# A hybrid decoder layer: the level products of three recurrent heads on 64-column halves of the array

## The chip, the core and the metric

One core of a Trainium2 chip runs the whole layer as one program. Its engines work side by side, each through its own queue in order: TensorE (matrix products; PE in the profile, its weight loads PEld), VectorE (DVE), ScalarE (ACT), GpSimd (POOL) and SyncE (SP), which issues most DMAs. The metric is the device time of the program in microseconds, median of three runs. Lower is better.

## The reference, cut to what matters

The layer is a mixer (eight heads of dilated attention beside four heads of a gated linear recurrence) and a feed-forward block. The change is in the recurrence. For one head and chunks of 64 positions:

```python
def step(state, xs):
    qc, kc, vc, gc = xs
    b = jnp.cumsum(gc, axis=2)
    o_inter = jnp.einsum('bhtk,bhkv->bhtv', qc * jnp.exp(b), state)
    diff = b[:, :, :, None, :] - b[:, :, None, :, :]
    decay = jnp.exp(jnp.where(causal, diff, -jnp.inf))
    a = jnp.einsum('bhtk,bhsk,bhtsk->bhts', qc, kc, decay)
    o = o_inter + jnp.einsum('bhts,bhsv->bhtv', a, vc)
    ...
```

The matrix `a` holds, for each query t and each earlier key s of its chunk, their product weighted by the decay between them, which differs in each of the 128 dimensions. There are 1024 positions, 128 dimensions a head, and everything is float32.

## The kernel before, in words

Positions are taken in eight tiles of 128, so that a tile holds two chunks of 64. The kernel keeps queries `qt` and keys `kt` of a head with the dimensions on the partitions and the positions along the row, and `tot`, the decay of each position.

**The levels.** The decayed products are not built one pair at a time. At level c the positions are cut in blocks of c. The products between the second block of each pair of blocks (queries) and the first (keys) are one matrix product, after which the queries and keys are multiplied by the decay of the block that they must now reach across. Levels 1, 2, 4, ... 32 fill a chunk, level 64 couples the two chunks of a tile, and the state carries what is further back.

Heads 0 to 2 take two levels, c and 2c, in one step, with c = 1, 4, 16 (`hgrn_core`, L502). For a step `quarter_sets` (L470) builds three sets of 64 queries a tile: one for level c, one for level 2c with the far half of the keys, one for the near half. Side by side they are the 192 columns of `qs`. One product a tile takes the tile's 128 keys as stationary operand and these 192 columns as moving operand (L529), and gives `pl`, 128 keys by 192 queries, in PSUM: eight products a step, two tiles to a bank. A key of the first chunk meets queries of both chunks there, and only those of its own chunk at the right blocks are wanted. DVE picks them out with `copy_predicated` (L561) into `at`, a table of 128 keys by 128 queries a tile, by masks: `masks` for the two levels, `near` for the set that couples at the smaller distance. Both masks are made once, near the start (L379 to L383), on DVE. `near` is followed there by `lb` and, by way of ACT, by the gates of head 0.

`at` begins as the diagonal (L511: the identity times a row of sums from `pd`). Level 64 is a product of its own, on 64 keys (L572), which ACT copies into the upper right quarter of `at` (L574). Then `at` is the stationary operand of the product that gives the head's output (L643). The last head takes the levels one by one (L593, L604).

**What sets the order.** The program is written out by hand: each engine runs its instructions in the order in which the code issues them. Projections of the next head (`pig`, `pm_q`, `pm_f`) and of the attention (`pm_aq`) stand in a queue of generators. Between the parts of a head, `fill(ns)` takes matrix products from it until the nanoseconds written there are used up. After each step it is called twice with 3500 times a scale. Between them `table_part` loads parts of the bias tables and turns them on POOL (`tout`, L718, L720). PSUM has eight banks in four pairs ("mm", "s", "t", "pv"); before, the four banks of `pl` of a step come from two of these pairs, in turn.

The masks come from an input of seven levels (`mraw`); `lowhalf` says for each key and step whether it lies in the second block at level c, and `near` is the mask of level 2c for those keys alone.

Of the kernel before, what the change touches and what calls it, by code (L numbers as in the profile page):

```python
# [10 lines left out]
U8 = mybir.dt.uint8  # L11
AF = mybir.ActivationFunctionType
# [25 lines left out]
def hymba_layer(ctx, tc, x, w_in, w_out, w_ff1, w_ff2, g_pre, lb_logits, g_mix, g_post,  # L38
# [26 lines left out]

    ident = cp.tile([P, P], F32, name="ident")
    masks = cp.tile([P, len(LEVELS), 64], U8, name="masks")
    near = cp.tile([P, 3, 64], U8, name="near")
    gpre = cp.tile([P, NK], F32, name="gpre")
    lbl = cp.tile([P, HH, 2], F32, name="lbl")  # L70
    lb = cp.tile([P, HH], F32, name="lb")
# [197 lines left out]
    def new_head(h):  # L269
        return {"inat": slab("T", f"inat{h}", F32, (P, NT, P)), "gate": slab("T", f"gate{h}", F32, (P, NT, P))}  # L270

    heads = [None] * HH
    heads[0] = new_head(0)

# [101 lines left out]
    for q in (2, 3):  # L376
# [3 lines left out]
    first = col("lowhalf", 3)  # L380
    V.tensor_reduce(first, mraw[:, 0:6].rearrange("p (s two) j -> p s two j", two=2)[:, :, 0], axis=AX.X, op=ALU.max)
    V.tensor_scalar(first, first, -1.0, 1.0, op0=ALU.mult, op1=ALU.add)
    V.tensor_tensor(out=near, in0=mraw[:, 0:6].rearrange("p (s two) j -> p s two j", two=2)[:, :, 1],  # L383
                    in1=first.unsqueeze(2).to_broadcast([P, 3, 64]), op=ALU.mult)
    V.tensor_tensor(out=lb, in0=lbl[:, :, 0], in1=lbl[:, :, 1], op=ALU.subtract)
    S.activation(omlb, lb, AF.Sigmoid, scale=-1.0)
    S.activation(lb, lb, AF.Sigmoid)
# [113 lines left out]
    def hgrn_core(h, scale, after=None):  # L501
# [5 lines left out]
        for hf in range(2):  # L507
            pd = bank("pv", f"pd{h}_{hf}")
            for q in range(2):
                TE.matmul(pd, ones.to_broadcast([P, P]), prod[q][:, hf * 512:hf * 512 + 512], start=q == 0, stop=q == 1)  # L510
            V.tensor_tensor(out=at[:, hf * 4:hf * 4 + 4], in0=ident.unsqueeze(1).to_broadcast([P, 4, P]),  # L511
                            in1=pd.rearrange("p (n c) -> p n c", n=4), op=ALU.mult)
        if h == 0:
            make_picks()
            nc.sync.dma_start(out=gcols, in_=g_mix.rearrange("(k p) -> p k", p=P))
# [2 lines left out]
        if h < HH - 1:  # L518
            fill(1200 * scale)
            totals = slab("P", f"tot{h}")  # L520
            for step in range(3):
                c = 4 ** step
                nb = 32 // c
                sets, cv = ready
                banks4 = []
                for u in range(4):
                    pl = bank(("s", "t", "pv")[(2 * step + u // 2) % 3], f"pl{h}_{step}{u}").rearrange("p (n q) -> p n q", n=2)
                    for n in range(2 * u, 2 * u + 2):
                        TE.matmul(pl[:, n % 2, :192], kt[:, n * P:(n + 1) * P], sets[u // 2][:, n % 4],  # L529
                                  start=True, stop=True)  # L530
                    banks4.append(pl)
                w = T // (4 * c)
                at_ = (0, 768, 960)[step]
                tots = totals[:, at_:at_ + 3 * w].rearrange("p (i w) -> p i w", i=3)
                u23, u123, nx = (tots[:, i] for i in range(3))
                cw = cv.rearrange("p n b f -> p (n b) f")
                q4 = qt.rearrange("p (m f c) -> p m f c", f=4, c=c)
                k4 = kt.rearrange("p (m f c) -> p m f c", f=4, c=c)

                def spread(ap, k=c):  # L540
                    return ap.unsqueeze(2).to_broadcast([P, w, k])
                V.tensor_tensor(out=q4[:, :, 1], in0=q4[:, :, 1], in1=spread(cw[:, :, 0]), op=ALU.mult)
                for hf in range(2):
                    n4 = slice(hf * 4, hf * 4 + 4)
                    V.tensor_tensor(out=qt[:, hf * 512:hf * 512 + 512].rearrange("p (n b f c) -> p n b (f c)", n=4, f=4, c=c)
                                    [:, :, :, 2 * c:],
                                    in0=sets[hf][:, :, 128:].rearrange("p n (b w) -> p n b w", b=nb),
                                    in1=cv[:, n4, :, 0:1].to_broadcast([P, 4, nb, 2 * c]), op=ALU.mult)
                V.tensor_tensor(out=u23, in0=cw[:, :, 2], in1=cw[:, :, 3], op=ALU.mult)
                V.tensor_tensor(out=u123, in0=cw[:, :, 1], in1=u23, op=ALU.mult)  # L550
                V.tensor_tensor(out=nx, in0=cw[:, :, 0], in1=u123, op=ALU.mult)
                if step < 2:
                    ready = quarter_sets(hd, h, step + 1, nx)
                V.tensor_tensor(out=k4[:, :, 2], in0=k4[:, :, 2], in1=spread(cw[:, :, 3]), op=ALU.mult)
                V.tensor_tensor(out=k4[:, :, 1], in0=k4[:, :, 1], in1=spread(u23), op=ALU.mult)
                V.tensor_tensor(out=k4[:, :, 0], in0=k4[:, :, 0], in1=spread(u123), op=ALU.mult)
                for u, pl in enumerate(banks4):
                    for part_, mask, c2 in ((0, masks[:, 2 * step], c), (2, masks[:, 2 * step + 1], 2 * c),
                                            (1, near[:, step], 2 * c)):
                        av = at[:, 2 * u:2 * u + 2].rearrange("p n (b two c) -> p n b two c", two=2, c=c2)  # L560
                        V.copy_predicated(  # L561
                            av[:, :, :, 1, :],
                            mask.rearrange("p (b c) -> p b c", c=c2).unsqueeze(1).to_broadcast([P, 2, 64 // c2, c2]),
                            pl[:, :, part_ * 64:part_ * 64 + 64].rearrange("p n (b c) -> p n b c", c=c2))
                cur = nx
                table_part()
                fill(3500 * scale)
                table_part()
                fill(3500 * scale)
            pl = bank("s", f"pl{h}_6")  # L570
            for n in range(NT):
                TE.matmul(pl[:64, n * 64:(n + 1) * 64], kt[:, n * P:n * P + 64], qt[:, n * P + 64:(n + 1) * P],  # L572
                          start=True, stop=True)
            S.activation(at[:64, :, 64:], pl[:64].rearrange("p (n c) -> p n c", n=NT), AF.Copy)  # L574
            kv, qv = (x.rearrange("p (n two c) -> p n two c", two=2, c=64) for x in (kt, qt))
            cv = cur.rearrange("p (n two) -> p n two", two=2)
            V.tensor_tensor(out=qv[:, :, 1], in0=qv[:, :, 1], in1=cv[:, :, 0:1].to_broadcast([P, NT, 64]), op=ALU.mult)
            V.tensor_tensor(out=kv[:, :, 0], in0=kv[:, :, 0], in1=cv[:, :, 1:2].to_broadcast([P, NT, 64]), op=ALU.mult)
            nx = tp.tile([P, NT], F32, tag="tot8", name=f"tot{h}_8", bufs=1)
            V.tensor_tensor(out=nx, in0=cv[:, :, 0], in1=cv[:, :, 1], op=ALU.mult)  # L580
            cur = nx
            fill(3400 * scale)
        else:
            cur = tot
            fill(1200 * scale)
            for li, c in enumerate(LEVELS):
                nb = 64 // c
                qv = qt.rearrange("p (b two c) -> p b two c", two=2, c=c)
                kv = kt.rearrange("p (b two c) -> p b two c", two=2, c=c)
                av = at.rearrange("p n (b two c) -> p n b two c", two=2, c=c)  # L590
                pl = bank("s", f"pl{h}_{li}")
                for n in range(NT):
                    TE.matmul(pl[:, n * 64:(n + 1) * 64], kt[:, n * P:(n + 1) * P],  # L593
                              qv[:, n * nb:(n + 1) * nb, 1, :], start=True, stop=True)
                w = T // (2 * c)
                cv = cur[:, :2 * w].rearrange("p (b two) -> p b two", two=2)
                V.tensor_tensor(out=kv[:, :, 0, :], in0=kv[:, :, 0, :],
                                in1=cv[:, :, 1:2].to_broadcast([P, w, c]), op=ALU.mult)
                V.tensor_tensor(out=qv[:, :, 1, :], in0=qv[:, :, 1, :],
                                in1=cv[:, :, 0:1].to_broadcast([P, w, c]), op=ALU.mult)  # L600
                nx = slab("P", f"tot{h}_{w}") if w > 32 else \
                    tp.tile([P, w], F32, tag=f"tot{w}", name=f"tot{h}_{w}", bufs=1)
                V.tensor_tensor(out=nx[:, :w], in0=cv[:, :, 0], in1=cv[:, :, 1], op=ALU.mult)
                V.copy_predicated(  # L604
                    av[:, :, :, 1, :],
                    masks[:, li].rearrange("p (b c) -> p b c", c=c).unsqueeze(1).to_broadcast([P, NT, nb, c]),
                    pl.rearrange("p (n b c) -> p n b c", n=NT, c=c))
                cur = nx
                fill((3700 if li == 0 else 2900 if li < 3 else 2200) * scale)
# [57 lines left out]
            gated(g2)  # L667


    halves = ((0, 64), (64, 128))  # L670
    pairs = [None] * (AH // 2)
    v_dram = [dp.tile([DIL, T // DIL, 4 * 64], F32, name=f"vd{pr}") for pr in range(AH // 2)]
    table_dram = [dp.tile([P, 4 * P + FAR], F32, name=f"tabd{hd}") for hd in range(AH)]
# [1638 lines left out]
```

## Time and profile before

| what | value |
|---|---|
| time, median of 3 runs | 1205.64 us (1205.62 to 1205.76) |
| the profiled execution: span from first to last instruction | 1203.5 us (the page gives no other time for it) |
| granted TensorE clock, mean | 0.999 |
| level products L529, PE | 144 records, 68.4 to 213.5 us |
| level-64 products L572, PE | 48 records, 99.0 to 222.2 us |
| masked copies L561, DVE | 108, 76.1 to 218.2 us |
| POOL and ACT busy | 294.7 us and 542.3 us |

How to read it: a float32 product of 128 by 192 appears as two matmul records and two weight loads (144 records for 72 products). A row of the timeline gives the start, the time until the last one's end, the engine, the line, the operation, what it writes and reads, and how many were merged. In "128*128 128x192" the first pair is the rows and columns of the array that the stationary operand takes, the second the moving operand. The ends of matmuls are modelled, so the distances between starts say more than the durations. In square brackets stands the idle time of the engine before the row, and what ended it.

### The profile page before, as it was taken

The page shows a single profiled execution, that of the slowest core. Times are in us where ns is not written, and L with a number is a line of the kernel's source. Part 1 is how long each engine was busy: PE and PEld are TensorE (multiplying, and loading weights), DVE is VectorE, ACT ScalarE, POOL GpSimd, SP SyncE. Part 2 cuts the span into 40 slices and gives each one's busy share as a digit, 9 for nine tenths or more (in the row PEclk, how much of TensorE's full clock was granted, in tenths as well). Part 3 has the DMA queues.
Part 4 walks back from the last instruction along what each step waited for, and adds up shares of the span by engine and source line. Part 5 has one row for each costly group of instructions (what it writes and reads, how often), then busy time and mean ns, then how long its engine had stood idle before and what let it go on. Part 6 is the DMA issues. An engine that isn't in the chain of part 4 may idle for free.

```text
span 1203.5 us, 17310 instructions
## 1 busy us (share of the span) xinstructions
PE 1195.3 (99%) x6342; PEld 1025.7 (85%) x6342; DVE 849.7 (71%) x1438; ACT 542.3 (45%) x1065; POOL 294.7 (24%) x280
## 2 busy tenths in 40 slices
PE   9999999999999999999999999999999999999997
PEld 9898989888888888888888888888888888888886
DVE  5696978775666767676599665766687553578796
ACT  7633333321565668855664222222234543434562
POOL 0121112010111110153421787575531000000022
PEclk9999999999999999999999999999999999999999
DMA  5222323135545556272524465553587534523337
GB/s 218 71 68 84 96 85 95 50 100 123 156 107 129 130 150 153 57 244 103 192 75 163 165 229 184 182 206 135 201 326 269 183 105 140 173 89 105 105 105 279
DMA packets 90547, 175.46 MB, mean 146 GB/s; under 512 B 14944, under 2 KB 42464, under 8 KB 90464
## 3 DMA queue, kind: packets, MB, share of 16 engines
q1 hardware_dynamic: 90320, 174.37, 45.6%
q8 instruction: 50, 0.82, 0.3%
q14 instruction: 33, 0.27, 0.1%
q10 hardware_dynamic: 144, 0.00, 0.0%
HBM read 116.91 MB, written 47.99 MB: 137 GB/s over the span
## 4 chain that ended last, share of the span: by engine, by line
PE 96%; ACT 2%; DVE 1%; issue 1%; DMA 0%; POOL 0%; DVEq 0%; POOLq 0%; ACTq 0%
PE f L2052 18%; PE f2s L2052 7%; PE pig L92 2%; PE pig L90 2%; PE pig L91 2%; PE pl L529 2%; PE pwo L90 2%; PE pwo L92 2%; PE pwo L91 2%; PE pm_ak L90 1%; PE pm_aq L90 1%; PE pm_f L90 1%; PE pm_aq L92 1%; PE pm_ak L92 1%; PE pm_ak L91 1%; PE pm_aq L91 1%
## 5 line engine op out<-in xcount | busy, mean ns | idle before, releaser
L87 DVE TENSOR_TENSOR al<-ar,ah 128x1024 fp32r<-128x1024 f32 x56 | 70.6, 1261 | 80.4 <-ACT ah L86 80.2
L2052 PE MATMUL f<-bh,ah 128*128 128x512 f32 x320 | 124.5, 389 | 0.0
L2052 PE MATMUL f<-bl,ah 128*128 128x512 f32 x320 | 124.5, 389 | 0.0
L2052 PE MATMUL f<-bh,al 128*128 128x512 f32 x320 | 124.5, 389 | 0.0
L86 ACT ACTIVATE ah<-ar 128x1024 fp32r<-128x1024 f32 x56 | 59.1, 1056 | 86.6 <-DMA ar<-actd 84.3
L2052 PEld LDWEIGHTS f<-bl,ah 128*128 128x128 f32 x320 | 60.1, 188 | 12.6
L2052 PEld LDWEIGHTS f<-bh,al 128*128 128x128 f32 x320 | 60.1, 188 | 12.5
L2052 PEld LDWEIGHTS f<-bh,ah 128*128 128x128 f32 x320 | 60.1, 188 | 12.3
L2126 POOL TENSOR_SCALAR lbl<-ssq 128x1 f32<-128x1 f32 x4 | 3.3, 820 | 245.7 <-ACT fd L2122 245.5
L1675 POOL TENSOR_TENSOR e<-x,e 128x512 f32<-128x512 f32 x14 | 21.6, 1541 | 131.0 <-DVE x L1626 123.8
L2052 PE MATMUL f2s<-bl,ah 128*128 128x512 f32 (+1 forms) x128 | 48.9, 382 | 0.0
L2052 PE MATMUL f2s<-bh,al 128*128 128x512 f32 (+1 forms) x128 | 48.9, 382 | 0.0
L2052 PE MATMUL f2s<-bh,ah 128*128 128x512 f32 (+1 forms) x128 | 48.9, 382 | 0.0
L718 POOL TENSOR_SCALAR tout<-traw 128x256 f32<-128x256 f32 x16 | 18.4, 1150 | 107.0 <-DMA traw<-in_bias_tab_dram 107.0
L87 DVE TENSOR_TENSOR bl<-br,bh 128x1024 fp32r<-128x1024 f32 x32 | 40.1, 1253 | 1.3 <-ACT bh L86 1.2
L2069 ACT ACTIVATE acc<-f 128x512 f32<-128x512 f32 x28 | 16.7, 598 | 49.5 <-PE f L2052 49.5
L86 ACT ACTIVATE bh<-br 128x1024 fp32r<-128x1024 f32 x32 | 33.6, 1050 | 4.3 <-PE f L2052 2.7
L87 DVE TENSOR_TENSOR wl<-raw,wh 128x1024 fp32r<-128x1024 f32 x21 | 25.9, 1233 | 10.2 <-ACT wh L86 10.2
L764 POOL TENSOR_TENSOR kl<-kf,kh 64x512 fp32r<-64x512 f32 x12 | 15.4, 1287 | 70.9 <-ACT kh L763 49.4
L90 PE MATMUL pwo<-woh,mt 128*128 128x512 f32 x80 | 32.2, 402 | 0.0
L92 PE MATMUL pwo<-woh,mt 128*128 128x512 f32 x80 | 31.3, 391 | 0.0
L91 PE MATMUL pwo<-wol,mt 128*128 128x512 f32 x80 | 31.2, 390 | 0.0
(1724 smaller groups left out, 3937.7 us busy)
## 6 DMA issues: line engine op xcount, KB each, us to landing
ar<-actd SPq DMA_DIRECT2D x56, 512.0 KB, 3.6
br<-in_w_ff_dram SPq DMA_DIRECT2D x16, 1024.0 KB, 5.8
raw<-in_w_in_dram SPq DMA_DIRECT2D x28, 512.0 KB, 4.1
w1r<-in_w_ff_dram SPq DMA_DIRECT2D x14, 1024.0 KB, 6.5
actd<-e SPq DMA_DIRECT2D x17, 768.0 KB, 4.3
actd<-e SPq DMA_DIRECT2D x11, 1024.0 KB, 4.1
xr<-in_x_dram SPq DMA_DIRECT2D x8, 512.0 KB, 8.0
raw<-in_w_out_dram SPq DMA_DIRECT2D x8, 512.0 KB, 3.7
```

Of the source, the lines that this page charges most:

```text
L86: S.activation(hi, src, AF.Copy)
L87: eng.tensor_tensor(out=lo, in0=src, in1=f32(hi), op=ALU.subtract)
L90: TE.matmul(dst, lhs[0], rhs[0], start=start, stop=False)
L91: TE.matmul(dst, lhs[0], rhs[1], start=False, stop=False)
L92: TE.matmul(dst, lhs[1], rhs[0], start=False, stop=stop)
L529: TE.matmul(pl[:, n % 2, :192], kt[:, n * P:(n + 1) * P], sets[u // 2][:, n % 4], start=True, stop=True)
L718: G.tensor_scalar(by_class(dst[:, part_ * w:(part_ + 1) * w]), in_blocks(raw[:, FAR * DIL:]), 8.0, None, op0=ALU.mult)
L764: G.tensor_tensor(out=kl[a:b], in0=src, in1=f32(kh[a:b]), op=ALU.subtract)
L1675: eng[0].tensor_tensor(out=e1[:, 3], in0=a21, in1=e1[:, 2], op=ALU.add)
L2052: TE.matmul(pm, a[:, j, c], b[:, j, d], start=start and j == 0 and q == 0, stop=stop and j == 1 and q == 2, skip_group_check=True)
L2069: S.activation(acc_at(p, i), pm, AF.Copy)
L2126: G.tensor_scalar(base[:, t:t + 1], sums[j][:, t:t + 1], 1.0 / D, EPS, op0=ALU.mult, op1=ALU.add)
```

## The change

For heads 0 to 2 a tile's 128 keys are taken as two halves of 64, one for each chunk. Each half is a stationary operand of 64 columns, and meets only the queries of its own chunk: 32 of each set of 64, thus 96 columns. The first half's result goes to PSUM partitions 0 to 63, that of the second to 64 to 127, which puts the one product on the left 64 columns of the array and the other on the right. There are twice as many products, each with half the keys and half the queries; four tiles fit one bank, so a step takes two banks, one pair of them ("s", "t", "pv" for the three steps).

`at` is kept compactly while the levels run: column j of a key's row is query j of the key's own chunk, so that 64 columns suffice. The masked copies then take 32 columns of four tiles where they took 64 columns of two, and there are six a step where there were twelve. The masks for this are `own` (both levels, six in all) and a `near` of half the width, built half by half. The diagonal is written by halves. At the end of the levels ACT copies the lower half of `at` to columns 64 to 127 and POOL clears what is left behind, so that the output product finds the same table as before. The last head is as it was, and its diagonal too.

```diff
-    near = cp.tile([P, 3, 64], U8, name="near")
+    own = cp.tile([P, 6, 32], U8, name="own")
+    near = cp.tile([P, 3, 32], U8, name="near")
...
-    V.tensor_tensor(out=near, in0=mraw[:, 0:6].rearrange("p (s two) j -> p s two j", two=2)[:, :, 1],
-                    in1=first.unsqueeze(2).to_broadcast([P, 3, 64]), op=ALU.mult)
+    for a, b, c in ((0, 64, 0), (64, P, 32)):
+        V.tensor_copy(own[a:b], mraw[a:b, 0:6, c:c + 32])
+        V.tensor_tensor(out=near[a:b], in0=mraw[a:b, 0:6].rearrange("p (s two) j -> p s two j", two=2)[:, :, 1, c:c + 32],
+                        in1=first[a:b].unsqueeze(2).to_broadcast([64, 3, 32]), op=ALU.mult)
...
-            V.tensor_tensor(out=at[:, hf * 4:hf * 4 + 4], in0=ident.unsqueeze(1).to_broadcast([P, 4, P]),
-                            in1=pd.rearrange("p (n c) -> p n c", n=4), op=ALU.mult)
+            pdv = pd.rearrange("p (n c) -> p n c", n=4)
+            if h == HH - 1:
+                V.tensor_tensor(out=at[:, hf * 4:hf * 4 + 4], in0=ident.unsqueeze(1).to_broadcast([P, 4, P]),
+                                in1=pdv, op=ALU.mult)
+                continue
+            for a, b in halves:
+                V.tensor_tensor(out=at[a:b, hf * 4:hf * 4 + 4, :64],
+                                in0=ident[a:b, a:b].unsqueeze(1).to_broadcast([64, 4, 64]),
+                                in1=pdv[a:b, :, a:b], op=ALU.mult)
...
-                for u in range(4):
-                    pl = bank(("s", "t", "pv")[(2 * step + u // 2) % 3], f"pl{h}_{step}{u}").rearrange("p (n q) -> p n q", n=2)
-                    for n in range(2 * u, 2 * u + 2):
-                        TE.matmul(pl[:, n % 2, :192], kt[:, n * P:(n + 1) * P], sets[u // 2][:, n % 4],
-                                  start=True, stop=True)
-                    banks4.append(pl)
+                got = []
+                for u in range(2):
+                    pl = bank(("s", "t", "pv")[step], f"pl{h}_{step}{u}").rearrange("p (n q) -> p n q", n=4)
+                    for n in range(4):
+                        qs = sets[u][:, n].rearrange("p (s w) -> p s w", s=3)
+                        for g, (a, b) in enumerate(halves):
+                            TE.matmul(pl[a:b, n, :96], kt[:, (4 * u + n) * P + a:(4 * u + n) * P + b],
+                                      qs[:, :, 32 * g:32 * g + 32], start=True, stop=True, skip_group_check=True)
+                    got.append(pl)
...
-                for u, pl in enumerate(banks4):
-                    for part_, mask, c2 in ((0, masks[:, 2 * step], c), (2, masks[:, 2 * step + 1], 2 * c),
+                for u, pl in enumerate(got):
+                    for part_, mask, c2 in ((0, own[:, 2 * step], c), (2, own[:, 2 * step + 1], 2 * c),
                                             (1, near[:, step], 2 * c)):
-                        av = at[:, 2 * u:2 * u + 2].rearrange("p n (b two c) -> p n b two c", two=2, c=c2)
+                        av = at[:, 4 * u:4 * u + 4, :64].rearrange("p n (b two c) -> p n b two c", two=2, c=c2)
...
+            S.activation(at[64:, :, 64:], at[64:, :, :64], AF.Copy)
+            G.memset(at[64:, :, :64], 0.0)
             S.activation(at[:64, :, 64:], pl[:64].rearrange("p (n c) -> p n c", n=NT), AF.Copy)
```

On TensorE's queue, at the first step of head 0, between two projections of head 1 (`pig`), stand before:

```order
L92 MATMUL pig_1_891<-wig1h,hTl_90 128x256
L529 MATMUL pl_00_905<-qs_00_808,kt_724 128x192 x2
L529 MATMUL pl_01_908<-qs_00_808,kt_724 128x192 x2
L529 MATMUL pl_02_911<-qs_01_813,kt_724 128x192 x2
L529 MATMUL pl_03_914<-qs_01_813,kt_724 128x192 x2
L90 MATMUL pig_1_891<-wig1h,hTh_91 128x256
```

and in the changed kernel, whose lines are numbered anew (L91 to L93 are the projections), at the same place:

```order
L93 MATMUL pig_1_897<-wig1h,hTl_91 128x256
L542 MATMUL pl_00_911<-qs_00_812,kt_728 64x96 x8
L542 MATMUL pl_01_920<-qs_01_817,kt_728 64x96 x8
L91 MATMUL pig_1_897<-wig1h,hTh_92 128x256
L92 MATMUL pig_1_897<-wig1l,hTh_92 128x256
```

The sizes are those of the result: eight products of 128 partitions by 192 have become sixteen of 64 by 96, in two banks, at the same place among the projections.

On DVE's queue, where the masks are made (`lowhalf`, `near`, and behind them `lb` and the gates and queries of head 0), stand before:

```order
L381 TENSOR_REDUCE lowhalf<-mraw 128x3
L382 TENSOR_SCALAR lowhalf<-lowhalf 128x3
L383 TENSOR_TENSOR near<-mraw,lowhalf 128x192
L385 TENSOR_TENSOR lb<-lbl 128x4
L267 TENSOR_TENSOR gate_143<-gate_143,sg_629 128x1024
L437 TENSOR_TENSOR qt_652<-pm_q_654,rrow 128x512
```

and in the changed kernel:

```order
L383 TENSOR_REDUCE lowhalf<-mraw 128x3
L384 TENSOR_SCALAR lowhalf<-lowhalf 128x3
L386 CAST own<-mraw 64x192
L387 TENSOR_TENSOR near<-mraw,lowhalf 64x96
L386 CAST own<-mraw 64x192
L387 TENSOR_TENSOR near<-mraw,lowhalf 64x96
L389 TENSOR_TENSOR lb<-lbl 128x4
L268 TENSOR_TENSOR gate_144<-gate_144,sg_633 128x1024
```

Four instructions stand ahead of `lb` where one stood.

More of the change, by code (lines that the diff above doesn't have):

```diff
@@ L270, in new_head @@
         return {"inat": slab("T", f"inat{h}", F32, (P, NT, P)), "gate": slab("T", f"gate{h}", F32, (P, NT, P))}
+    halves = ((0, 64), (64, 128))
     heads = [None] * HH
@@ L524, in hgrn_core @@
                 sets, cv = ready
-                banks4 = []
-                for u in range(4):
-                    pl = bank(("s", "t", "pv")[(2 * step + u // 2) % 3], f"pl{h}_{step}{u}").rearrange("p (n q) -> p n q", n=2)
-                    for n in range(2 * u, 2 * u + 2):
-                        TE.matmul(pl[:, n % 2, :192], kt[:, n * P:(n + 1) * P], sets[u // 2][:, n % 4],
-                                  start=True, stop=True)
-                    banks4.append(pl)
+                got = []
[7 more added lines that the diff above has]
+                    got.append(pl)
                 w = T // (4 * c)
@@ L556, in hgrn_core @@
                 V.tensor_tensor(out=k4[:, :, 0], in0=k4[:, :, 0], in1=spread(u123), op=ALU.mult)
-                for u, pl in enumerate(banks4):
-                    for part_, mask, c2 in ((0, masks[:, 2 * step], c), (2, masks[:, 2 * step + 1], 2 * c),
+                for u, pl in enumerate(got):
+                    for part_, mask, c2 in ((0, own[:, 2 * step], c), (2, own[:, 2 * step + 1], 2 * c),
                                             (1, near[:, step], 2 * c)):
-                        av = at[:, 2 * u:2 * u + 2].rearrange("p n (b two c) -> p n b two c", two=2, c=c2)
+                        av = at[:, 4 * u:4 * u + 4, :64].rearrange("p n (b two c) -> p n b two c", two=2, c=c2)
                         V.copy_predicated(
                             av[:, :, :, 1, :],
-                            mask.rearrange("p (b c) -> p b c", c=c2).unsqueeze(1).to_broadcast([P, 2, 64 // c2, c2]),
-                            pl[:, :, part_ * 64:part_ * 64 + 64].rearrange("p n (b c) -> p n b c", c=c2))
+                            mask.rearrange("p (b c) -> p b c", c=c2).unsqueeze(1).to_broadcast([P, 4, 32 // c2, c2]),
+                            pl[:, :, part_ * 32:part_ * 32 + 32].rearrange("p n (b c) -> p n b c", c=c2))
                 cur = nx
@@ L667, in hgrn_core @@
             gated(g2)
-    halves = ((0, 64), (64, 128))
     pairs = [None] * (AH // 2)
```

## The prediction

> **What bounds the kernel now.** I read the page first, then TensorE's waits, then the recurrent stretch by windows, then the start times around the instructions that are replaced.
>
> ```profile
> span 1203.5 us, 17310 instructions
> PE 1195.3 (99%) x6342; PEld 1025.7 (85%) x6342; DVE 849.7 (71%) x1438; ACT 542.3 (45%) x1065; POOL 294.7 (24%) x280
> PE 96%; ACT 2%; DVE 1%; issue 1%; DMA 0%; POOL 0%; DVEq 0%; POOLq 0%; ACTq 0%
> 68.00:98.00 30.00, 30.00 (x213) 28.96 (x212) 27.73 (x77) 7.67 (x22) 8.59 (x8) 1.00 0.35 94
> PEld pl L572 <- issue: 1.1, 3, 0.4
> PEld pm_f L90 <- DVE qt L437: 0.3, 1, 0.3
> ```
>
> TensorE is busy for 99% of the span and makes 96% of the chain that ended last. Its weight loads wait for others a few times, by tenths of a microsecond (the last two rows are two of the longer ones). In the first head's level steps (68 to 98 us; the columns are PE, PEld, DVE, ACT, POOL, clock, DMA) PE never stops at full clock, and DVE is busy 27.73 of 30 us beside it, without holding it up. So the time is the sum of PE's start-to-start distances. What PE saves or pays in a head reaches the end one to one; what DVE saves is worth nothing by itself.
>
> PE's ends are modelled, so I price by starts. Three groups in the timeline of PE, each with its neighbours:
>
> ```profile
> 68.21 0.28 PE L91 MATMUL pig<-wig1l,hTh 128*128 128x256 f32 x1
> 68.32 0.28 PE L92 MATMUL pig<-wig1h,hTl 128*128 128x256 f32 x1
> 68.44 2.76 PE L529 MATMUL pl<-qs,kt 128*128 128x192 f32 x16
> 70.91 0.42 PE L90 MATMUL pig<-wig1h,hTh 128*128 128x256 f32 x1
> 71.17 0.28 PE L91 MATMUL pig<-wig1l,hTh 128*128 128x256 f32 x1
> ...
> 98.44 0.39 PE L91 MATMUL pm_q<-hTl,wh 128*128 128x512 f32 x1
> 98.67 0.39 PE L92 MATMUL pm_q<-hTh,wl 128*128 128x512 f32 x1
> 98.98 1.15 PE L572 MATMUL pl<-qt,kt 128*64 128x64 f32 x16
> 100.06 0.50 PE L90 MATMUL pm_q<-hTh,wh 128*128 128x512 f32 x1
> 100.39 0.39 PE L91 MATMUL pm_q<-hTl,wh 128*128 128x512 f32 x1
> ...
> 251.57 0.39 PE L92 MATMUL pm_aq<-hTh,wl 128*128 128x512 f32 x1
> 251.80 1.89 PE L593 MATMUL pl<-qt,kt 128*128 128x64 f32 x16
> 253.50 0.48 PE L90 MATMUL pm_aq<-hTh,wh 128*128 128x512 f32 x1
> 253.82 0.39 PE L91 MATMUL pm_aq<-hTl,wh 128*128 128x512 f32 x1
> ```
>
> Each fp32 product is two records, so eight products make 16. **L529** (the products that change): from the last pig start before (68.32) to the second pig start behind (71.17) are 2.85 us; two pig distances of 0.12 (68.21 to 68.32) come off: 2.61 us, 0.163 a record. **L593** (the last head, 128 keys against 64 columns): 251.57 to 253.82 is 2.25, less two distances of 0.23 (98.44 to 98.67, the same form): 1.79 us, 0.112 a record. A third of the columns does not take a third of the time: here the load of 128 weight columns sets the pace. **L572** (64 keys against 64 columns, on 64 columns of the array): 98.67 to 100.39 is 1.72, less two 0.23: 1.26 us.
>
> ```profile
> 98.98 1.01 PEld L572 LDWEIGHTS pl<-qt,kt 128*64 128x64 f32 x16 [0.35 <-issue]
> L572 PEld LDWEIGHTS pl<-qt,kt x48: 132/138/138, 99.0 to 222.1; 128*64 128x64 f32 x48
> L529 PE MATMUL pl<-qs,kt x144: 323/326/328, 68.4 to 213.5; 128*128 128x192 f32 x144
> ```
>
> Its 16 loads of 0.138 each span 1.01 us, so they start (1.01 - 0.138) / 15 = 0.058 apart: half of L593's 0.112 for half the columns. 16 x 0.058 is 0.93; the other 0.33 of 1.26 us is lost going from 128 to 64 columns and back, as the load's wait of 0.35 for "issue" shows. L593, which stays on 128 columns, has nothing left over.
>
> The trace thus agrees with the Trainium skill, TensorEngine Tiling (Array Packing), Key Properties: a change of tiling mode drains TensorE, while a change of tile within a mode does not.
>
> **The change on PE.** The x144 row is nine groups (three heads, three steps) of 16 records. Each becomes 32 records of 64 keys against 96 columns, on the two column halves in turn: left, left, right, right. One record streams half of L529's columns: 0.163 / 2 = 0.081 (estimate; by proportion from L572's 0.058 for 64 columns it is 0.087). Each group now goes into the 64-column mode and out: +0.33. No row shows two halves at work in turn, so the pace is bounded:
> - Below: both halves stream at once and loads cost nothing more: 32 x 0.081 / 2 = 1.30, with 0.33 1.63 us against 2.61; 9 x 0.98 = 8.8 us saved.
> - Above: one after the other as on the full array: 32 x 0.081 = 2.59, with 0.33 2.92; 9 x 0.31 = 2.8 us lost (4.5 with 0.087). The bounds come from L529 and L572; that a switch of halves costs extra is a rival below.
> - I take the value of the nearest row: the halves stream at once, but 64-column loads come 0.058 apart, as in L572, the only row in this mode: 32 x 0.058 = 1.86, with 0.33 2.19; 9 x 0.42 = **3.8 us saved**.
>
> The Trainium skill, TensorE: Matmul & The Clock Gate, Part 3 (Packing small matmuls), gives 2.38x for three 32-column tiles at N=512, starts some 4 ns apart; no run here shows it. Taken as 1.6x for two halves (an estimate from it), the group would take 1.95 us and the nine would save 5.9 us. The sum stays at 3.8.
>
> **DVE ahead of the first level.** The old near (L383) becomes four instructions, own and near for each half of the partitions:
>
> ```profile
> 44.61 0.39 DVE L379 CAST masks<-mraw 128x448 uint8<-128x448 f32 x1
> 44.91 0.35 DVE L381 TENSOR_REDUCE lowhalf<-mraw 128x3 f32<-128x192 f32 x1
> 45.30 0.17 DVE L382 TENSOR_SCALAR lowhalf<-lowhalf 128x3 f32<-128x3 f32 x1
> 45.50 0.36 DVE L383 TENSOR_TENSOR near<-mraw,lowhalf 128x192 uint8<-128x192 f32 x1
> 45.78 0.15 DVE L385 TENSOR_TENSOR lb<-lbl 128x4 f32<-128x4 f32 x1
> 47.39 1.23 DVE L267 TENSOR_TENSOR gate<-gate,sg 128x1024 f32<-128x1024 f32 x1 [1.46 <-ACT sg L266]
> 48.53 0.68 DVE L437 TENSOR_TENSOR qt<-pm_q,rrow 128x512 f32<-128x512 f32 x1
> 45.97 0.21 ACT L386 ACTIVATE omlb<-lb 128x4 f32<-128x4 f32 x1 [1.23 <-DVE lb L385]
> ```
>
> Every link is tight: lb lets ACT go on after 1.23 us of waiting, ACT's sg (queued behind omlb) lets DVE's gate go on after 1.46, qt follows, and PE's pm_f waits 0.3 us for qt (the row in the first fence). So whatever is put ahead of lb moves PE. By distances between starts, 3 elements cost 0.20, 192 cost 0.28 and 448 cost 0.30: four instructions of 96 and 192 lie between 4 x 0.20 and 2 x 0.30 + 2 x 0.28, less the 0.28 that goes: +0.5 to +0.9. I take **+0.6 us**, low in the band, since size matters little and the first copy need not wait for lowhalf.
>
> **What hides.**
>
> ```profile
> L561 DVE COPY_PREDICATED at<-masks,pl x72: 281/301/500, 76.1 to 217.9; 128x128 f32<-128x128 uint8 x72
> L561 DVE COPY_PREDICATED at<-near,pl x36: 292/304/452, 77.1 to 218.2; 128x128 f32<-128x128 uint8 x36
> L511 DVE TENSOR_TENSOR at<-ident,pd x8: 678/680/681, 67.8 to 254.1; 128x512 f32<-128x512 f32 x8
> L574 ACT ACTIVATE at<-pl x3: 592/592/596, 100.2 to 222.5; 64x512 f32<-64x512 f32 x3
> 103.78 1.10 POOL L718 TENSOR_SCALAR tout<-traw 128x256 f32<-128x256 f32 x1 [7.13 <-DMA traw<-in_bias_tab_dram]
> 112.05 0.64 PEld L643 LDWEIGHTS po<-inat,at 128*128 128x128 f32 x4
> ```
>
> The 108 masked copies become 54 of the same 128 elements: about 54 x 0.30 = 16 us less DVE work, under PE all along, counted as nothing. It also means that a faster PE does not run into DVE: PE gains at most 2.9 us a head, DVE 5.4. The diagonal goes from two writes of 512 elements to four of 256 a head, at most 4 x 0.68 - 2 x 0.68 = 1.4 us of DVE, paid from those 5.4. At the end of a head ACT copies 64x512 (0.6 us, as L574) and POOL clears as much; behind ACT's copy wait only the level-64 copy and ktr. POOL's memset stands behind the last table part (103.78 + 1.10 = 104.9) and should be done by 106.0, if it is no dearer than that part; PE first reads at at 112.05. If the table's DMA came 6 us later, PE would wait. SP has the same rows in the same order.
>
> **Sum.** -3.8 + 0.6 = -3.2 us on a span of 1203.5. The page gives no other time for its execution; the three runs (median 1205.64) lie 2.1 us above that span, and I carry this along: **1202.4 us**. A measurement of this kernel tells about 0.2%, 2.4 us, from no change.
>
> **Rivals.**
> - *Full overlap* (chance 0.27): loads of the two halves go side by side too. -8.8 + 0.6: 1197.4. For it: in L529 loads hide wholly behind streams (0.163 is kept although 128-column loads need 0.112). Against it: no row has two loads at once.
> - *Strict order* (0.14): the right half's load starts only when the second left record has started, so records come 0.081 and 0.058 apart in turn: 16 x 0.139 + 0.33 = 2.55, -0.5 + 0.6: 1205.7. For it: PEld and PE records alternate strictly.
> - *The halves do not overlap* (0.19): the change then does not do what it says, and the mode costs 0.33 a group: +2.8 to +4.5, + 0.6: 1209.0 to 1210.7, slower. It decides once a record costs over 0.071 on average ((2.61 - 0.33) / 32). For it: no row shows two streams at once.
> - *Each change of half stalls the array, or loads lie bare* (0.10): a stall of half the 0.33 at 16 changes adds 2.6 us a group, 24 us in all on the serial case: 1233. With bare loads each record costs 0.058 + 0.081, 32 x 0.139 + 0.33 = 4.78, 9 x 2.17 + 0.6 = +20: 1225.8. Against bare loads: on full rows L529's loads hide.
>
> The Trainium skill, TensorE: Matmul & The Clock Gate, Part 3, What overlaps, says that loads pass running matmuls only where the row group differs; both halves here use all rows, so by it loads lie bare. The trace disagrees for the full array.
>
> **How the numbers follow.** The forecast has 0.30. Faster: full overlap 0.27 and 0.24 of the forecast (0.06 of it falls short of 2.4 us), 0.51. Same: that 0.06, strict order 0.14, 0.02 of the serial case, 0.22. Slower: 0.17 of the serial case and 0.10, 0.27. The range runs from full overlap to the dear end of the serial case, 1197.0 to 1210.8, and leaves out the last rival.
>
> **What would show it.** 288 records of L529's successor on 64 columns; within a group loads 0.058 apart say the forecast, about 0.041 full overlap, 0.081 the serial case. A group should take 2.2 us between its neighbours, with 0.33 lost at its ends. PE's wait for qt at pm_f should grow from 0.3 to 0.9. DVE should be some 16 us less busy. Wrong would be: the halves' records never overlap, PE waits for at in front of po, or PE's waits for DVE grow elsewhere.

## The result, and the profile after

The changed kernel takes 1198.41 us (median of four runs, 1197.81 to 1199.92) against 1205.63 (1205.39 to 1205.76) for the kernel before: a ratio of 0.9942, 95% interval 0.9928 to 0.9956. That is 0.6% faster, and the span of the profiled execution went from 1203.5 to 1195.6 us. The forecast was 1202.4; what came is, to 1.0 us, the first rival, full overlap, at 1197.4.

The page of the changed kernel, its span, its engines and its chain:

```profile
span 1195.6 us, 17551 instructions
PE 1186.2 (99%) x6486; PEld 1014.5 (85%) x6486; DVE 838.1 (70%) x1393; ACT 543.9 (45%) x1068; POOL 295.8 (25%) x283
PE 96%; ACT 2%; DVE 1%; DMA 1%; issue 1%; POOL 0%; DVEq 0%; POOLq 0%; ACTq 0%
```

PE is still busy 99% of the time and still 96% of the chain: only the sum of its distances has become smaller. The new level products, by tile and in PE's timeline at the first group:

```profile
L542 PEld LDWEIGHTS pl<-qs,kt x288: 132/137/137, 69.0 to 205.3; 128*64 128x64 f32 x144
L542 PE MATMUL pl<-qs,kt x288: 246/246/297, 69.0 to 205.4; 128*64 128x96 f32 x144
```

```profile
68.67 0.28 PE L92 MATMUL pig<-wig1l,hTh 128*128 128x256 f32 x1
68.79 0.28 PE L93 MATMUL pig<-wig1h,hTl 128*128 128x256 f32 x1
69.00 1.54 PE L542 MATMUL pl<-qs,kt 128*64 128x96 f32 x32
70.48 0.38 PE L91 MATMUL pig<-wig1h,hTh 128*128 128x256 f32 x1
70.70 0.28 PE L92 MATMUL pig<-wig1l,hTh 128*128 128x256 f32 x1
```

Read as the prediction read L529: 68.79 to 70.70 is 1.91, less two pig distances of 0.12: **1.67 us a group** where 2.61 stood. The starts of the 32 records show why. They come in pairs, 7 to 8 ns apart within a pair and 0.0825 from pair to pair:

```
69.004 69.011   69.138 69.145   69.220 69.228   69.303 69.310   69.385 69.393
```

16 pairs x 0.0825 = 1.32, and 0.35 more is lost going into the 64-column mode and out of it. The pace is that of one half streaming 96 columns; the other half runs beside it, and the loads cost nothing on top.

Over the whole program, the same PE instructions start this much later (+) or earlier (-) than before (from both traces, in us):

| place | at, before | offset |
|---|---|---|
| pm_f of head 0, behind the masks | 49.3 | +0.50 |
| behind the three groups of head 0 | 70.9, 81.1, 91.2 | -0.44, -1.38, -2.31 |
| behind those of head 1 | 132.4, 142.6, 152.7 | -3.30, -4.23, -5.17 |
| behind those of head 2 | 193.2, 203.4, 213.5 | -6.08, -7.01, -7.95 |
| from there to the end | | -7.95 |

So the whole change is nine steps of -0.94 and one of +0.50: -7.95, against 7.9 between the spans. Nothing else moves PE.

The one step that lost, in DVE's timeline, and PE's waits behind it:

```profile
45.31 0.17 DVE L384 TENSOR_SCALAR lowhalf<-lowhalf 128x3 f32<-128x3 f32 x1
45.39 0.24 DVE L386 CAST own<-mraw 64x192 uint8<-64x192 f32 x1
45.56 0.24 DVE L387 TENSOR_TENSOR near<-mraw,lowhalf 64x96 uint8<-64x96 f32 x1
45.82 0.26 DVE L386 CAST own<-mraw 64x192 uint8<-64x192 f32 x1
45.99 0.25 DVE L387 TENSOR_TENSOR near<-mraw,lowhalf 64x96 uint8<-64x96 f32 x1
46.27 0.16 DVE L389 TENSOR_TENSOR lb<-lbl 128x4 f32<-128x4 f32 x1
47.90 1.23 DVE L268 TENSOR_TENSOR gate<-gate,sg 128x1024 f32<-128x1024 f32 x1 [1.46 <-ACT sg L267]
49.04 0.68 DVE L441 TENSOR_TENSOR qt<-pm_q,rrow 128x512 f32<-128x512 f32 x1
```

```profile
PE pm_f L91 <- DVE qt L441: 0.5, 1, 0.5
PEld pm_f L91 <- DVE qt L441: 0.8, 1, 0.8
```

`lb` starts at 46.27 where it started at 45.78, and everything in the chain behind it is 0.5 us later: the gate (47.39 to 47.90), the queries (48.53 to 49.04), PE's loads, whose wait grows from 0.3 to 0.8.

### The profile page after: what moved, and what is told of

Its sections match the earlier page's. It is cut to its first block, busy times and chain, and to the rows that moved or that the text cites. A ratio compares the mean times of both kernels' runs of the same rounds, so it can differ in the third digit from the quotient of the medians.

```text
span 1195.6 us, 17551 instructions
## 1 busy us (share of the span) xinstructions
PE 1186.2 (99%) x6486; PEld 1014.5 (85%) x6486; DVE 838.1 (70%) x1393; ACT 543.9 (45%) x1068; POOL 295.8 (25%) x283
## 4 chain that ended last, share of the span: by engine, by line
PE 96%; ACT 2%; DVE 1%; DMA 1%; issue 1%; POOL 0%; DVEq 0%; POOLq 0%; ACTq 0%
PE f L2066 18%; PE f2s L2066 7%; PE pig L91 3%; PE pig L93 2%; PE pig L92 2%; PE pwo L93 2%; PE pwo L91 2%; PE pwo L92 2%; PE pm_aq L91 1%; PE pm_f L91 1%; PE pm_ak L91 1%; PE pm_aq L93 1%; PE pm_aq L92 1%; PE pm_f L93 1%; PE pm_f L92 1%; PE pm_ak L93 1%
## 5 line engine op out<-in xcount | busy, mean ns | idle before, releaser
L91 PE MATMUL pwo<-woh,mt 128*128 128x512 f32 x80 | 32.2, 402 | 0.0
L93 PE MATMUL pwo<-woh,mt 128*128 128x512 f32 x80 | 31.3, 391 | 0.0
```

The costliest lines, as they stand in the source:

```text
L91: TE.matmul(dst, lhs[0], rhs[0], start=start, stop=False)
L93: TE.matmul(dst, lhs[1], rhs[0], start=False, stop=stop)
```

## The experiments

Spans are compared with the changed kernel's 1195.6; "offset" is again the start of the same PE instruction against it. The four executions of the changed kernel had spans of 1195.6 to 1197.5 us, and the profiled one is the shortest; E1 and E8 ran four times, the others once. A difference under 2 us is therefore read from the places where PE's starts step, and not from a span alone. E3, E2 and E4 ask where the 0.94 us a group come from, E5 and E9 what DVE's saving is for, E1, E6, E7, E8 and E10 what more there is.

### E3: all products on the left half

```diff
-                            TE.matmul(pl[a:b, n, :96], kt[:, (4 * u + n) * P + a:(4 * u + n) * P + b],
+                            TE.matmul(pl[:64, n, :96], kt[:, (4 * u + n) * P + a:(4 * u + n) * P + b],
```

(The masked copies then read and write 64 partitions, and the results of the right keys are left out.)

> The changed kernel with all products on the left half of the array; the results of the right keys are left out (they overwrite the left ones, and only partitions 0 to 63 are taken by the masked copies). It prices the same 32 records without a second half. Theory (the gain is the overlap of the halves): records 0.0825 us apart, group 3.0 us, +11 to +12 us against the changed kernel, some 4 us slower than before. Rival (the gain is that smaller products are cheaper in themselves): group stays near 1.7 us, no change.

Measured: 1209.97 us, span 1207.6, +12.0. PE's timeline at the first group:

```profile
68.74 0.28 PE L92 MATMUL pig<-wig1l,hTh 128*128 128x256 f32 x1
68.95 2.85 PE L542 MATMUL pl<-qs,kt 128*64 128x96 f32 x32
71.74 0.39 PE L91 MATMUL pig<-wig1h,hTh 128*128 128x256 f32 x1
71.96 0.28 PE L92 MATMUL pig<-wig1l,hTh 128*128 128x256 f32 x1
```

68.74 to 71.96 less 0.24 is 2.98 us: the same 32 records, one behind the other, 32 x 0.0825 + 0.35 = 2.99. The whole gain, and 0.37 us a group more, is the second half of the array working beside the first. Halving the work of a record without a place for the other half is a loss of 4 us against the kernel before. It also shows that on one half the loads of 64 columns are hidden behind streams of 96, so that the pace of 0.0825 is that of the stream.

### E2: four left products, then four right ones

```diff
-                    for n in range(4):
-                        qs = sets[u][:, n].rearrange("p (s w) -> p s w", s=3)
-                        for g, (a, b) in enumerate(halves):
+                    for g, (a, b) in enumerate(halves):
+                        for n in range(4):
+                            qs = sets[u][:, n].rearrange("p (s w) -> p s w", s=3)
```

> The changed kernel with the four left products of a bank first, then the four right ones. Theory (the halves overlap only with a neighbour in the queue): eight records of one side stand in a row and run one after the other, 0.0825 us apart, so a group takes about 32 x 0.0825 + 0.35 = 3.0 us instead of 1.67 and the span grows by 9 x 1.2 to 1.3, about 11 us, against the changed kernel. Rival (the array looks far ahead and starts whatever half is free): no change. In between: a look-ahead of a few records overlaps the ends of the two runs only, +9 to +10 us.

Measured: 1202.50 us, span 1200.2, +4.6, which is 0.51 a group: the right sign, and about half of the size foretold. The level records in the first 0.4 us of the first group, of the changed kernel and of E2, by tile:

```profile
L542 PE MATMUL pl<-qs,kt x10: 246/246/297, 69.0 to 69.4; 128*64 128x96 f32 x10
```

```profile
L542 PE MATMUL pl<-qs,kt x5: 246/246/297, 69.1 to 69.4; 128*64 128x96 f32 x5
```

and the starts that follow in E2:

```
69.066   69.199   69.281   69.364   69.446 69.452   69.529   69.586 69.611   69.669 69.694
```

Four starts stand alone, 0.08 apart and more, and then the sixth comes 6 ns behind the fifth. Records on one half start 0.082 apart (E3), so one of the two must be on the right half, where the first record stands ninth in the program. The durations point the same way: of the 32 records of a group one lasts 297 ns and the rest 246 where one half is used (E3), and two where both are (the changed kernel), always the first of its half; in the first group of E2 four last 297: the first, the sixth and those at 69.840 and 70.226, where the sides take turns again. So TensorE starts a record ahead of some three earlier ones that wait for the other half, but not ahead of seven; whether it is the load or the stream that may pass only so many, no run separates. The Trainium skill, TensorE: Matmul & The Clock Gate, Part 3, What overlaps, says that matmuls start and end strictly in the order of the program; these starts, so read, disagree. What the order costs here is 0.5 us a group; in the changed kernel, where the halves alternate every two records, nothing is left to gain from another order.

### E4: into the mode and out of it twice

```diff
                     got.append(pl)
+                    if u == 0:
+                        fill(1.0, True)
```

This puts one piece of a projection, three matmuls on the full array, between the two banks of a step.

> The changed kernel with one piece of the projections (three full-array products) between the two banks of each step, so that the array goes into the 64-column mode and out twice a step instead of once. Theory (each entry and exit costs about 0.35 us): +9 x 0.35 = +3.1 us against the changed kernel. Rival (the 0.35 belongs to the wait for VectorE at the first product, not to the mode): nothing, within 0.3 us.

Measured: 1202.10 us, span 1199.8, +4.2. PE's timeline at the first group:

```profile
68.85 0.28 PE L93 MATMUL pig<-wig1h,hTl 128*128 128x256 f32 x1
69.07 0.88 PE L542 MATMUL pl<-qs,kt 128*64 128x96 f32 x16
69.88 0.38 PE L91 MATMUL pig<-wig1h,hTh 128*128 128x256 f32 x1
70.10 0.28 PE L92 MATMUL pig<-wig1l,hTh 128*128 128x256 f32 x1
```

68.85 to 70.10 less 0.24 is 1.01 for 16 records: 8 x 0.0825 + 0.35. Two such runs take 2.02 where one of 32 took 1.67, so nine of them cost 9 x 0.35 = 3.15. The other 1.0 us is a side effect: the pieces are taken earlier, and later PE stands in front of `pd` without cover. PE's waits:

```profile
PEld pd L514 <- DVE prl L465: 1.1, 2, 0.5
```

The price of 0.33 that the prediction took from L572 is the price of the mode. That going in and out costs time at all agrees with the Trainium skill, TensorEngine Tiling (Array Packing), Key Properties; the 0.35 us is measured here.

### E5 and E9: masked copies put back

In E5 each of the 54 copies is made twice, in E9 only those of the first of the two banks (81 copies in all):

```diff
-                for u, pl in enumerate(got):
+                for u, pl in ((u, pl) for u, pl in enumerate(got) for _ in range(2)):
```

```diff
-                for u, pl in enumerate(got):
+                for u, pl in ((u, pl) for u, pl in enumerate(got) for _ in range(2 - u)):
```

> The changed kernel with each of the six masked copies of a step made twice (the second writes the same values again), so that VectorE has its old 108 copies. Theory (what VectorE saves is worth nothing, the gain is TensorE's alone): VectorE some 16 us busier, span within 0.5 us of the changed kernel's. Rival (part of the 7.9 us comes from VectorE being less loaded): the span grows by 1 us or more and TensorE shows new waits for VectorE's keys or queries ahead of the level products.

Measured: 1207.25 us, span 1205.0: +9.4, slower than the kernel before. The prediction's sentence that "what DVE saves is worth nothing by itself" does not carry over to the changed kernel: with the faster PE, part of DVE's saving is needed. (What it would be worth beside the old, slower PE, no run asks.) E5's waits:

```profile
PE pk L630 <- DVE kt L593: 4.8, 3, 1.9
PE pl L542 <- DVE kt L569: 2.1, 3, 1.0
PEld pk L630 <- DVE kt L593: 6.1, 3, 2.4
```

In the changed kernel none of these is among PE's waits. DVE rescales the keys `kt` at the end of each step ahead of the copies of that step, so the copies of one step delay the keys of the next; PE needs those keys for the next product and, at the end of a head, for their transposition `pk`. In the second head more comes behind the wait, in PE's timeline and in the windows (PE, PEld, DVE, ACT, POOL, granted clock, DMA):

```profile
164.76 1.09 PE L630 MATMUL pk<-ident,kt 128*128 128x128 f32 x8 [1.94 <-DVE kt L593]
165.61 0.57 PE L91 MATMUL pm_f<-hTh,wh 128*128 128x512 f32 x1
165.97 0.63 PE L92 MATMUL pm_f<-hTl,wh 128*128 128x512 f32 x1
166.40 0.63 PE L93 MATMUL pm_f<-hTh,wl 128*128 128x512 f32 x1
```

```profile
162.00:166.00 4.00, 2.06 (x14) 1.50 (x13) 2.68 (x6) 2.44 (x5) 0.00 (x0) 0.98 0.52 164
166.00:170.00 4.00, 4.00 (x12) 3.17 (x11) 2.70 (x3) 2.90 (x5) 1.63 (x2) 0.59 0.00 0
```

After PE had stood for 1.94 us the granted clock falls to 0.59 for the next four, and the projections start 0.43 apart (165.97 to 166.40) instead of 0.23: 1.7 us more. The waits at `pk` in the other two heads were shorter, 1.38 and 1.52 us, and brought no lower clock.

That left open whether DVE has a reserve that E5 used up, or whether each copy slows PE in proportion:

> Only the first of the two tiles' copies are made twice: 81 copies, 2.7 us more DVE work a head than the changed kernel, where all 108 brought 5.4 us and cost PE 2.3 to 2.6 us of waiting for kt a head, and 1.7 us of a lower clock in the second. Theory: DVE has about 3 us a head in hand before PE waits for its kt, and only what goes beyond that is paid. Then 2.7 us a head cost nearly nothing: span 1195.6 to 1196.6, and PE does not wait for kt at pk. Rival: each copy slows PE by itself (they read the banks that PE writes), so that half of the copies costs half: about +4.7, span 1200.3, with PE's records longer or waits spread over the groups.

Measured: 1198.62 us, span 1196.2, +0.6. PE's waits:

```profile
PE pl L542 <- DVE kt L569: 0.3, 1, 0.3
```

Half of the copies cost 0.6 us, all of them 9.4: it is a reserve, with an edge. DVE is busy 838.1 us in the changed kernel, 846.6 in E9, 855.4 in E5, and was 849.7 before. The edge lies between E9 and E5; so does the load of the kernel before, and what its copies would have cost the faster PE, between 0.6 and 9.4 us, is not measured.

Where the edge is met can be read from the traces, as the time from the end of the last rescaling of `kt` to the first load of the product that uses it. A load that waits for the keys starts 0.12 us behind them. In the changed kernel the loads of the second step start 0.82, 0.81 and 0.15 us behind (heads 0 to 2), where it was 2.26, 2.16 and 1.48 before: in head 2 the reserve is used up already, and E9 waits just there. At the third step 2.05 to 3.05 us are left; E5 brings this to 0.12 in all three heads.

### E1: lb ahead of the masks

```diff
+    V.tensor_tensor(out=lb, in0=lbl[:, :, 0], in1=lbl[:, :, 1], op=ALU.subtract)
     V.tensor_copy(masks, mraw)
...
-    V.tensor_tensor(out=lb, in0=lbl[:, :, 0], in1=lbl[:, :, 1], op=ALU.subtract)
```

> The changed kernel with lb put ahead of all mask work on VectorE; nothing else moves. Theory (the masks stand in the chain lb, omlb, sg, gate, qt, pm_f): ScalarE can start sg some 1.6 us earlier, TensorE's wait for qt at the first pm_f goes from 0.8 us to nothing, and the span falls by about 0.75 us against the changed kernel (0.5 of it the price of the four mask instructions, the rest the old wait). Rival (the chain is held by something else at this place, such as the row scales that qt also reads): the wait stays and the span with it.

Measured: 1197.45 us (1197.12 to 1198.65), ratio to the kernel before 0.9936 (0.992 to 0.9953), span 1194.9. DVE's timeline, and PE's waits:

```profile
44.54 0.15 DVE L381 TENSOR_TENSOR lb<-lbl 128x4 f32<-128x4 f32 x1
46.26 1.23 DVE L268 TENSOR_TENSOR gate<-gate,sg 128x1024 f32<-128x1024 f32 x1
47.41 0.68 DVE L441 TENSOR_TENSOR qt<-pm_q,rrow 128x512 f32<-128x512 f32 x1
```

```profile
PE pl L542 <- DVE kt L569: 0.2, 1, 0.2
```

The gate no longer waits, `qt` comes 1.6 us earlier, and PE starts pm_f 0.9 us earlier. Of this 0.3 is lost again in the second step of head 2, where PE now meets DVE's keys (0.15 us were left there). The intervals of the two ratios overlap; the step in PE's starts does not leave the sign in doubt, but the gain of 0.7 us in the spans is smaller than the spread of the changed kernel's own runs.

### E6, E7, E8 and E10: more of the same

E6 sends the level-64 products to the two halves in turn:

```diff
-                TE.matmul(pl[:64, n * 64:(n + 1) * 64], kt[:, n * P:n * P + 64], qt[:, n * P + 64:(n + 1) * P],
-                          start=True, stop=True)
+                a, b = halves[n % 2]
+                TE.matmul(pl[a:b, n // 2 * 64:n // 2 * 64 + 64], kt[:, n * P:n * P + 64], qt[:, n * P + 64:(n + 1) * P],
+                          start=True, stop=True, skip_group_check=True)
```

> The changed kernel with the level-64 products of heads 0 to 2 (64 keys against 64 columns, all on the left half) put on both halves in turn, one tile left and the next right; ScalarE then takes two copies for one. Theory (two halves stream and load at once, whatever the size): 16 records go from 0.058 to 0.029 us each, 3 x 0.46 = 1.4 us less span. Rival (records bound by their loads, as these are, do not overlap): no change.

Measured: 1196.50 us, span 1194.3, -1.3. PE's timeline at head 0:

```profile
96.44 0.39 PE L93 MATMUL pm_q<-hTh,wl 128*128 128x512 f32 x1
96.76 0.69 PE L586 MATMUL pl<-qt,kt 128*64 128x64 f32 x16
97.38 0.50 PE L91 MATMUL pm_q<-hTh,wh 128*128 128x512 f32 x1
97.71 0.39 PE L92 MATMUL pm_q<-hTl,wh 128*128 128x512 f32 x1
```

96.44 to 97.71 less two distances of 0.23 is 0.81, where L572 took 1.26: 8 x 0.058 + 0.35. If these records go at the pace of their loads, as the prediction read L572, that pace too is had twice at once. It is a narrow call: a stream of 64 columns would be 0.056, an estimate by a straight line through the 0.1625 of 192 columns (L529) and the 0.0825 of 96.

E7 cuts the first two steps of a head into 32 keys against 48 columns on quarters of the array (and has lb first, and the masks of the halves and quarters made by POOL). Its core:

```diff
+                        for a in range(0, P, 32):
+                            TE.matmul(pl[a:a + 32, n, :48], kt[:, n * P + a:n * P + a + 32],
+                                      qs[:, :, a // 2:a // 2 + 16], start=True, stop=True, skip_group_check=True,
+                                      tile_position=(0, a))
```

> Steps c = 1 and c = 4 of heads 0 to 2 on quarters of the array: 32 keys against the 48 queries of their own 32 positions, four column tiles in turn, one bank a step, the table kept in 32 columns until the third step; the masks are made on GpSimd and lb comes first on VectorE. Theory (as many column tiles run at once as there are): 64 records a step in 16 slots of 0.0425, 0.68 us instead of 1.32, 6 x 0.64 = 3.8 us less, with about 0.7 for lb first 4.5 us below the changed kernel. Rival (TensorE looks only some three records ahead, as the trace with the sides apart suggests, and the fourth quarter stands six records behind the first): two to three tiles at once, between 0 and 2 us less, with 0.7 for lb.

Measured: 1195.72 us, span 1193.9, -1.7: well short. PE's timeline at the first group, and PE's waits:

```profile
68.18 0.28 PE L95 MATMUL pig<-wig1h,hTl 128*128 128x256 f32 x1
68.39 0.89 PE L552 MATMUL pl<-qs,kt 128*32 128x48 f32 x64
69.21 0.39 PE L93 MATMUL pig<-wig1h,hTh 128*128 128x256 f32 x1
69.43 0.28 PE L94 MATMUL pig<-wig1l,hTh 128*128 128x256 f32 x1
```

```profile
PE pl L552 <- DVE kt L588: 2.6, 3, 1.3
```

The group itself does what was foretold: 68.18 to 69.43 less 0.24 is 1.01, or 16 rounds of four records at 0.0425, as their starts show, and 0.33 for the mode. But in the second step of each head PE now waits up to 1.3 us for the keys of the first. The offsets gain about 0.6 in the first step of a head, nothing in the second of heads 0 and 1, and lose 0.76 there in head 2. So DVE's edge is met here too. PE came earlier, but DVE also came later, as its diagonal shows, in E7 and in E1, which has lb first as well:

```profile
67.63 2.36 DVE L529 TENSOR_TENSOR at<-ident,pd 32x128 f32<-32x128 f32 x8
```

```profile
67.31 1.71 DVE L521 TENSOR_TENSOR at<-ident,pd 64x256 f32<-64x256 f32 x4
```

Eight pieces take 0.65 us more than four, and they start 0.3 later: the keys of head 0's second step are ready at 77.46, against 76.45 in E1, where PE loaded them at 77.29. PE 0.66 us earlier than that would still have met E1's keys. So in head 0 it is mostly the quarters' own work on DVE that takes their gain; in head 2, where E1 had no reserve left, PE's gain alone would have met the keys too. No run separates the two.

E8 is E7 and E6 together.

> Quarters, masks on GpSimd with lb first, and the level-64 products on both halves together. Theory (the parts add on TensorE): 3.8 + 0.7 + 1.4 = 5.9 us below the changed kernel, about 1192.5 us. Rival (look-ahead limits the quarters): 1194.5 to 1196.5 us. VectorE, with fewer copies, should not be waited for.

Measured: 1194.54 us (1194.16 to 1194.63), ratio to the kernel before 0.9909 (0.9893 to 0.9926), span 1192.4: -3.2 against the changed kernel, the sum of E6's 1.3 and E7's 1.7 within 0.2, and short of the 5.9 foretold where E7 fell short. It is the fastest of these kernels. E10 leaves the quarters out and keeps lb first and level 64 on both halves:

> Halves as in the changed kernel, lb first and the level-64 product on both halves, without quarters. Theory: the two edits add up, 0.7 and 1.3 us: span 1193.6, and the quarters of the kernel that had all three are worth 1.2 us. Rival: a faster level 64 makes PE wait for kt at pk, as lb first did in the last head, and the sum falls short: 1194.3.

Measured: 1195.98 us, span 1193.8, -1.8. PE's starts are 0.6 earlier behind the masks and 0.46 at each level 64, 2.0 in all, less 0.3 at the wait for `kt` that E1 had met already, in the second step of head 2 and not at `pk` as the rival had it. The sum comes nearer to the first theory than to the rival. The quarters, as they are built here, are worth 1.4 us (one run of E10 against E8), for a good deal of code.

## Why the prediction was right or wrong

- **What bounds it.** That what PE saves in a head reaches the end one to one held: the nine steps and the one loss add up to the difference of the spans.
- **The pace of a record** is the term that was mis-sized. The prediction took 0.058 us, since L572 was the only row on 64 columns, and its loads come 0.058 apart. That row had all its loads on one half. The runs show 0.041 (0.0825 for a pair, E3 the same 0.0825 for one), so a group took 1.67 instead of 2.19, and nine of them -8.4 instead of -3.8. That loads come one after another had been inferred from a row in which no other half was there to be loaded. The lower bound of 1.63, half of L529's stream for each record and the mode, was the nearest value. The time lies within the range only because the range reaches to full overlap: the forecast itself had less than half of the gain, and its choice between the bounds was the wrong one.
- **The mode**: 0.33 taken, 0.35 measured, by E4 in a direct way. That a change of half within the mode costs nothing, no row of the kernel before could show, as it used one half alone; the starts 7 to 8 ns apart show it now.
- **DVE ahead of lb**: +0.6 priced, +0.50 measured; the wait at pm_f grew to 0.8 (0.9 foretold).
- **What hides.** The compact `at` is ready long before it is read, as the rows by tile show:

```profile
L588 POOL MEMSET at<- x3: 519/519/522, 101.4 to 213.5; 64x512 f32 x3
L658 PEld LDWEIGHTS po<-inat,at x64: 187/192/192, 109.7 to 292.3; 128*128 128x128 f32 x64
```

  POOL clears it from 101.4 on (104.9 to 106.0 was foretold), and in each head it is done seven us or more ahead of the first load. DVE is 11.6 us less busy where 16 was foretold. The masked copies do give the 16 (33.5 to 17.2 us, overlapping time counted once), the diagonal takes 1.2 of it back and `own` 0.4; the rest lies in DVE instructions that the change leaves alone, the queries' `qt<-qt,tot` above all (16.0 to 17.2), and was not followed up. DVE's saving counted as nothing, and E5 and E9 show that the changed kernel needs part of it; the remark beside it, that DVE's 5.4 us a head keep PE from running into DVE, was what mattered, though at the second step of head 2 only 0.15 us were left.
- **The rivals.** Strict order, no overlap and bare loads are all excluded by the 1.67 us. By the page of the Trainium skill that the prediction weighed (TensorE: Matmul & The Clock Gate, Part 3, What overlaps), loads pass running matmuls only where the row group differs; here both halves use all rows, and the trace disagrees: the pair of records costs one stream of 0.0825, and no load shows beside it.

## What to carry to other kernels

In these runs a product that left half of its results unused could be split by columns of the stationary operand: with the two halves fed in turn, a group took its rounds times the longer of one half's stream and load, and a fixed 0.35 us for each entry into the mode and exit. A price for such a step must come from a row in which both halves work, or be bounded as if loads and streams were had twice. And when PE gets faster, look at what DVE hands to it in the same stretch: its idle time is a reserve with an edge, and a saving there can be what makes the saving on PE count.

## What the runs showed of the hardware

- Records on different column halves start 7 to 8 ns apart, and four on quarters run together: a pair takes 0.0825 us with 96 columns, four take 0.0425 with 48 (E7), and a pair 0.058 with 64 (E6), which the prediction read as the pace of the load.
- TensorE starts a record ahead of some three earlier ones that wait for the other half of the array (E2), but no further.
- A wait of 1.94 us on PE was followed by some four us at a granted clock of 0.59 on the mean; waits of 1.38 and 1.52 us at the same place in the other heads were not (E5).
